# Where the per-token scale of a gated MLP is applied, and one more Strassen product, in a two-layer encoder trunk

## The chip, the core and the metric

The kernel runs on one core of a Trainium2 chip. The metric is the device time of one execution in microseconds (us); lower is better. The engines are called as the profile calls them: PE is TensorE (matrix products), PEld its weight loads, DVE is VectorE, ACT is ScalarE, POOL is GpSimd, and SP issues the DMAs.

## What is computed

The reference is a trunk of two layers over 512 tokens of width 1024. Each layer adds a mixer (differential attention in layer 0, gated linear attention in layer 1, with cross-attention into 256 memory tokens beside it) and then a gated MLP with a causal convolution of width 3. Only the MLP is touched here:

```python
def rms_norm(x, g):
    y = xf * lax.rsqrt(jnp.mean(xf * xf, axis=-1, keepdims=True) + EPS)
    return (y * g)

def conv_ffn(h, w_up, conv_w, conv_b, w_down):
    u = h @ w_up                       # 1024 -> 2 * 2816
    c = depthwise_causal_conv(u, conv_w) + conv_b
    a, g = jnp.split(c, 2, axis=-1)
    return (jax.nn.silu(g) * a) @ w_down
...
        h = rms_norm(x, ffn_norm[i])
        x = x + conv_ffn(h, w_up[i], conv_w[i], conv_b[i], w_down[i])
```

The norm's factor, one number per token, can be applied to the tokens ahead of `w_up` or, since the product is linear, to every result behind it.

## The kernel before

Everything is kept transposed: a tile is 128 features by 512 tokens in float32. The stream `xT[0..7]` is eight such tiles. A factor of a product is split into a high and a low part in the type fp32r (`parts_of`, `split`, `split_weights`: ACT rounds to the high part, DVE subtracts to get the low part), and a product is three matmuls, high by high, high by low, low by high (`product`, lines 407 to 409).

In the MLP (`ffn`) the 2816 hidden features are worked on in eleven groups `q` of 256, the halves `n` of 128 each. For each half there is a linear piece `ua` and a gate piece `ug`; their results stand in one PSUM bank each (`take` deals the eight banks in the order of `TURNS`). `conv` reads a bank: line 1248 multiplies it in place by `rB`, the token factor spread over all partitions, ACT starts the convolution with the middle tap and the bias (1250), and two DVE instructions add the other taps (1251, 1252). Then ACT applies silu to the gate (1455), DVE multiplies (1457), and the hidden tile is split into `mid` parts (1278, 1279). After groups 0 to 3, 4 to 7 and 8 to 10 (`HALVES`) `down` multiplies the hidden tiles into the stream, by Strassen's scheme with seven products of 128 by 256 for what would be eight (line 1358).

Strassen's scheme needs sums of blocks on both sides. Sums of weight blocks are made by POOL (`block_sums`, line 285) and split (308 to 312). Sums of hidden tiles are `mid_sums`, on POOL for most groups and on DVE for the last of a part (line 1286). Sums of tokens are `token_sums`; they need the tokens with the feature gain, made by `scaled` on ACT (line 1321), four POOL subtractions per pair of tiles (1286 with `wsum`), and a split into `vs` parts. `SEVEN` lists the up pieces that use the scheme: groups 5, 6, 8 and 9 of `ua` in each layer and one `ug` piece (`up_by_seven`, line 1233). In such a piece the tiles 6 and 7 go in plainly and the other three pairs of tiles by seven products; four banks hold the partial results, which are combined on ACT and DVE (1238 to 1244). `SUMS_AT` says after which half (2q + n) the sums of which pair of tokens are made.

DVE, ACT and POOL take their instructions from queues in order. The order of PE is the order of the code; the order of the others is set by a planner at build time, which may pull an instruction ahead, except where `keep_in_program_order` fixes it, as on POOL. Weight tiles are made up to six slots ahead (`WB`; a block of a Strassen piece takes two slots, a plain block one), the tag `cvo` has seven buffers, `wsum` two, `vs` twelve, `xs` thirty-six.

Of the kernel before, what the change touches and what calls it, by code (L numbers as in the profile page):

```python
# [14 lines left out]
AF = mybir.ActivationFunctionType  # L15
ALU = mybir.AluOpType
# [69 lines left out]
def _pieces():  # L86
# [3 lines left out]
    def piece(key, name, i, ks, *ranges):  # L90
        plan.append((key, name, i, ks, ranges))

    for l in range(2):
# [24 lines left out]
        for nq in HALVES:  # L118
            for q in range(base, base + nq):
                for key, c in ((("ua", l, q), 256 * q), (("ug", l, q), DFF + 256 * q)):  # L120
                    piece(key, "w_up", l, (6, 7, 4, 5, 0, 1, 2, 3) if key in SEVEN else K8, (c, c + 256))
            for c in range(4):
# [14 lines left out]
    return out  # L137


SEVEN = (('ua', 0, 5), ('ua', 0, 6), ('ua', 0, 8), ('ua', 0, 9), ('ua', 1, 5), ('ua', 1, 6), ('ua', 1, 8), ('ua', 1, 9), ('ug', 0, 9))  # L140
SUMS_AT = {1:(4,5),2:(0,1),3:(2,3)}
TURNS = ('mm', 'mm', 'sm', 'sm', 'lg', 'lg', 'tp', 'tp')


# [40 lines left out]
def trunk(ctx, tc, head_d, x_t, mem_t, wpack, cols_a_d, cols_d, conv_d, gate_d, rel_bias, diff_lambda, consts, onehot, out):  # L185
    nc = tc.nc
    mm = nc.tensor.matmul
    V, A, G = nc.vector, nc.scalar, nc.gpsimd
# [9 lines left out]
    def bank(tag):  # L198
        return ps.tile([128, 512], F32, name=f"ps_{tag}", tag=tag)
# [4 lines left out]
    def split_tiles(pool=None, tag="xs", bufs=XS):  # L204
        pool = pool or xs
        return (pool.tile([128, S], F32R, name=tag + "h", tag=tag, bufs=bufs),
                pool.tile([128, S], F32R, name=tag + "l", tag=tag, bufs=bufs))
# [4 lines left out]
    def blk(b, w=128):  # L212
        return slice(w * b, w * b + w)
# [12 lines left out]
    def tables(name):  # L226
        tc.keep_in_program_order(A.preload_act_table_set(name))
# [94 lines left out]
    def by_seven(i):  # L322
        return plan[i][0][0] == "dn" or plan[i][0] in SEVEN

    def sum_tile():
        return sum_pool[0].tile([128, WTILE], F32, name="wsum", bufs=2)
# [37 lines left out]
    def split(hi, lo, src, gain):  # L364
        A.activation(hi, src, AF.Copy, scale=gain)
        V.scalar_tensor_tensor(lo, src, gain, hi.bitcast(F32), op0=ALU.mult, op1=ALU.subtract)  # L366
# [45 lines left out]
    xT = [None] * KT  # L412
# [12 lines left out]
    def col(i, t=cols):  # L425
        return t[:, i:i + 1]
# [3 lines left out]
    c_ffn = lambda l, k: col(8 * l + k)  # L430
# [70 lines left out]
    with tc.tile_pool(name="ini", bufs=1) as ip, tc.manual_schedule(engines={E.Activation, E.DVE, E.Pool, E.SP}):  # L501
# [8 lines left out]
        p = bank("tp")  # L510
# [48 lines left out]
        for k in range(KT):  # L559
# [17 lines left out]
            hi, lo = parts[k]  # L577
# [590 lines left out]
    def ffn(pool, l, acc):  # L1168
        rB = pool.tile([128, S], F32, name="rB", bufs=1)
        sum_pool[0] = pool  # L1170
        tokens, sums_of, nb = list(zip(xh, xl)), {}, [0]
# [14 lines left out]
        def begin(key):  # L1186
            nonlocal live
            assert plan[used[0]][0] == key, (plan[used[0]][0], key)
            used[0] += 1
            refill()  # L1190
            return used[0] - 1
# [16 lines left out]
        def ctile():  # L1208
            return pool.tile([128, S], F32, name="cvo", bufs=7)

        def up(i, n):
            p, = take(1)
            product(p, whole_piece(i), n, tokens)
            if n == 1:
                release(i, 2, True)
            return p

        def up_by_seven(i):
# [25 lines left out]
            V.tensor_add(b[1], b[1], w)  # L1244
            return b[:2]

        def conv(p, j):
            V.tensor_mul(p, p, rB)
            c = ctile()
            first = A.activation(c, p, AF.Identity, scale=cv[l][:, 2, j:j + 1], bias=cv[l][:, 3, j:j + 1])  # L1250
            V.scalar_tensor_tensor(c[:, 1:], p[:, :S - 1], cv[l][:, 1, j:j + 1], c[:, 1:], op0=ALU.mult, op1=ALU.add)
            final = V.scalar_tensor_tensor(c[:, 2:], p[:, :S - 2], cv[l][:, 0, j:j + 1], c[:, 2:], op0=ALU.mult, op1=ALU.add)
            if later:
                convs[0] += 1
                if convs[0] == (2):
                    convs[0] = 0
                    behind(first, final)
            return c
# [15 lines left out]
        def mid_tile():  # L1274
            return xs.tile([128, S], F32R, name="mid", tag="xs", bufs=XS)

        def parts_of(t, hi, lo):
            A.copy(hi, t)
            V.tensor_sub(lo, t, hi.bitcast(F32))

        def combine(b2, b1, E, t, parts):
            q = [blk(i, 256) for i in range(4)]
            at = lambda i: t[i // 2][:, q[i % 2]] if len(t) > 1 else t[0][:, q[i]]
            for i, x, y in ((0, b1[:, right], b1[:, left]), (1, b2[:, right], at(0)), (2, b2[:, right], b1[:, right]),
                            (3, b2[:, left], at(1))):
                ins = E.tensor_sub(at(i), x, y)  # L1286
                if E is G:
                    tc.keep_in_program_order(ins)
            parts(t)
            return q  # L1290

        def operands(h, lo, bh, bl, fh, fl):
            two = lambda hi, lw, c: (hi[:, c], lw[:, c])
            return [(fh, fl), two(bh, bl, left), two(bh, bl, right), (h[3], lo[3]), (h[0], lo[0]), (h[1], lo[1]),
                    (h[2], lo[2])]
# [16 lines left out]
        def behind(*ins):  # L1312
            with ExitStack() as stack:
                for i in ins:
                    stack.enter_context(tc.issue_after(i.ins))
                while later:
                    parts_of(*later.pop(0))

        def scaled(k):
            t = ctile()  # L1320
            A.activation(t, xT[k], AF.Copy, scale=c_ffn(l, k))
            return t

        def token_sums(ks):
            (bh, bl), (fh, fl) = (tokens[k] for k in ks)
            tiles = [split_tiles(pool, "vs", 12) for _ in range(2)]

            def parts(t):
                for i, (hi, lo) in enumerate(tiles):
                    parts_of(t[0][:, blk(i, S)], hi, lo)  # L1330
            combine(scaled(ks[0]), scaled(ks[1]), G, [sum_tile()], parts)
            h, lo = ([t[i][:, c] for t in tiles for c in (left, right)] for i in range(2))
            sums_of[ks] = operands(h, lo, bh, bl, fh[:, left], fl[:, left])
# [99 lines left out]
        for part, nq in enumerate(HALVES):  # L1433
            mids, pairs = [], []
            last = part == len(HALVES) - 1
            for q in range(base, base + nq):
                c2, ops, at, cs = [], [], {}, {}

                def half(key, n, j):
                    if n == 0:  # L1440
                        at[key] = begin((key, l, q))
                        if (key, l, q) in SEVEN:
                            cs[key] = [conv(p, j + i) for i, p in enumerate(up_by_seven(at[key]))]
                    if key in cs:
                        return lambda: cs[key][n]
                    p = up(at[key], n)
                    return lambda: conv(p, j + n)

                for n in range(2):
                    ua = half("ua", n, 2 * q)  # L1450
                    ug = half("ug", n, 22 + 2 * q)
                    if q == 0 and n == 0:
                        row_scales(acc[0])
                    cn, cg = ua(), ug()
                    A.activation(cg, cg, AF.Silu)
                    end = q == base + nq - 1
                    V.tensor_mul(cn, cn, cg)  # L1457
                    c2.append(cn)
                    if n == 0 or last:
                        ops += [mid_tile(), mid_tile()]  # L1460
                        parts_of(cn, *ops[-2:])
                        pairs.append(ops[-2:])
                    else:
                        m = mid_tile()
                        ops += [m[:, left], m[:, right]]
                        parts_of(cn[:, left], *ops[-2:])
                    if 2 * q + n in SUMS_AT:
                        token_sums(SUMS_AT[2 * q + n])
                if last:
                    ops[2:] = [t[:, left] for t in ops[2:]]  # L1470
                if not last or l == 1:
                    mids.append(mid_sums(c2, ops, V if end else G))
            acc2 = [None]
            if last and l == 0:
                tables("natural_log_exp_and_others")
                gw = gate_raw[0] = ctile()[:96, :384]
                G.memset(gw, 0.0)
                for b in range(3):
                    load(gw[32 * b:32 * b + 17], gate_d)
            down(base, nq, mids, pairs, last, acc2)  # L1480
            base += nq
# [87 lines left out]
```

## Time and profile before

| | |
|---|---|
| median of three runs | 1144.44 us (1144.1 to 1144.5) |
| the profiled execution, its own time | 1144.21 us |
| its span, first to last instruction | 1142.4 us |
| busy: PE, DVE, ACT, POOL | 1137.8, 934.7, 619.8, 279.5 us |
| the MLP of layer 0, of layer 1 (start of first up product to end of last) | 241 to about 559 us, 790 to about 1108 us, then the last `down` |
| granted TensorE clock | 1.0 throughout |

A window of the trace gives for a stretch of time how long each engine was busy in it. Busy time of PE counts a matmul from its start to its modelled end, and matmuls overlap, so the pace of PE is read from the starts in the timeline and not from durations. A group line gives an instruction's line, engine, output and inputs, its shape, its count, its total and mean time, and the idle time ahead of it with what ended that.

### The profile page before, as it was taken

To read this page: it belongs to the slowest core of one execution; us is meant where nothing else is said; L and a number is where in the kernel's file an instruction comes from. 1 tells how busy PE (TensorE), PEld (TensorE's weight loads), DVE (VectorE), ACT (ScalarE), POOL (GpSimd) and SP (SyncE) were. 2 spreads that over 40 slices of the span, in tenths; PEclk is the share of its full clock that TensorE was granted. 3 is DMA by queue.
4 is the path that set the end of the run, shared out by engine and by line. 5 is a ranking of instruction groups with operands and counts; after the bars stand their busy time and mean duration, and the time that the engine had idled before them with its cause. 6 is when DMAs were issued, how large, how long until landed. Compare 5 with 4: busy or idle time off the path is not lost.

```text
span 1142.4 us, 17519 instructions
## 1 busy us (share of the span) xinstructions
PE 1137.8 (100%) x6554; PEld 992.9 (87%) x6554; DVE 934.7 (82%) x1553; ACT 619.8 (54%) x1097; POOL 279.5 (24%) x326
## 2 busy tenths in 40 slices
PE   9999999999999999999999999999999999999998
PEld 7888888888899888999888888988888989899888
DVE  7676778689989899999777636778888988999997
ACT  6676687556554355445557634536664434544552
POOL 0000000004364425760000000000246432575240
PEclk9999999999999999999999999999999999999999
DMA  8522242132313332243252330234222243234312
GB/s 290 175 74 96 79 143 70 59 112 78 125 57 129 100 104 74 89 134 112 88 178 72 94 96 19 82 125 140 74 74 93 93 129 93 92 94 130 105 52 102
DMA packets 39666, 117.87 MB, mean 103 GB/s; under 512 B 4767, under 2 KB 7256, under 8 KB 39582
## 3 DMA queue, kind: packets, MB, share of 16 engines
q1 hardware_dynamic: 39150, 116.37, 32.1%
q8 instruction: 51, 0.84, 0.3%
q10 hardware_dynamic: 432, 0.39, 0.1%
q14 instruction: 33, 0.27, 0.1%
HBM read 112.54 MB, written 4.21 MB: 102 GB/s over the span
## 4 chain that ended last, share of the span: by engine, by line
PE 99%; DMA 0%; DVE 0%; issue 0%; SPq 0%; ACT 0%
PE ps_mm L407 6%; PE ps_mm L408 6%; PE ps_mm L409 6%; PE ps_mm L385 6%; PE ps_mm L387 6%; PE ps_mm L386 6%; PE ps_lg L1358 5%; PE ps_sm L407 4%; PE ps_sm L408 4%; PE ps_sm L409 4%; PE ps_mm L1358 4%; PE ps_tp L1358 4%; PE ps_sm L1358 3%; PE ps_tp L224 3%; PE ps_lg L1233 3%; PE ps_tp L408 3%
## 5 line engine op out<-in xcount | busy, mean ns | idle before, releaser
L260 DVE TENSOR_TENSOR wlo<-raw,whi 128x1024 fp32r<-128x1024 f32 (+5 forms) x165 | 185.9, 1139 | 76.4 <-ACT whi L257 74.2
L257 ACT CAST whi<-raw 128x1024 fp32r<-128x1024 f32 (+5 forms) x165 | 157.2, 967 | 101.2 <-PE ps_mm L408 20.3
L285 POOL TENSOR_TENSOR wsum<-raw 128x256 f32<-128x256 f32 (+1 forms) x112 | 99.6, 910 | 115.2 <-DMA raw<-in_wpack_dram 56.5
L385 PE MATMUL ps_mm<-whi,xsh 128*128 128x512 f32 (+2 forms) x328 | 126.4, 385 | 0.0
L387 PE MATMUL ps_mm<-whi,xsl 128*128 128x512 f32 (+2 forms) x328 | 123.1, 375 | 0.0
L386 PE MATMUL ps_mm<-wlo,xsh 128*128 128x512 f32 (+2 forms) x328 | 122.9, 375 | 0.0
L407 PE MATMUL ps_mm<-xsh,whi 128*128 128x512 f32 x294 | 115.6, 393 | 0.0
L408 PE MATMUL ps_mm<-xsl,whi 128*128 128x512 f32 x294 | 114.7, 390 | 0.0
L409 PE MATMUL ps_mm<-xsh,wlo 128*128 128x512 f32 x294 | 114.6, 390 | 0.0
L311 ACT CAST whi<-wsum 128x1024 fp32r<-128x1024 f32 (+1 forms) x56 | 53.6, 957 | 49.3 <-POOL wsum L285 43.7
L1286 POOL TENSOR_TENSOR cvo<-cvo 128x256 f32<-128x256 f32 x56 | 47.4, 866 | 134.3 <-DVE cvo L1457 133.2
L408 PE MATMUL ps_sm<-xsl,whi 128*128 128x512 f32 x202 | 78.7, 389 | 0.0
L407 PE MATMUL ps_sm<-xsh,whi 128*128 128x512 f32 x202 | 78.7, 389 | 0.0
L409 PE MATMUL ps_sm<-xsh,wlo 128*128 128x512 f32 x202 | 78.6, 389 | 0.0
L312 DVE TENSOR_TENSOR wlo<-wsum,whi 128x1024 fp32r<-128x1024 f32 (+1 forms) x56 | 67.1, 1198 | 7.1 <-ACT whi L311 5.6
L385 PEld LDWEIGHTS ps_mm<-whi,xsh 128*128 128x128 f32 x328 | 61.8, 188 | 11.4 <-issue 1.0
L387 PEld LDWEIGHTS ps_mm<-whi,xsl 128*128 128x128 f32 x328 | 61.7, 188 | 11.3
L386 PEld LDWEIGHTS ps_mm<-wlo,xsh 128*128 128x128 f32 x328 | 61.9, 189 | 10.1
L1263 POOL MEMSET xsh<- 128x128 f32 x2 | 0.4, 210 | 276.4 <-PE ps_sm L408 189.9
L409 PEld LDWEIGHTS ps_mm<-xsh,wlo 128*128 128x128 f32 x294 | 55.2, 188 | 11.6
L407 PEld LDWEIGHTS ps_mm<-xsh,whi 128*128 128x128 f32 x294 | 55.3, 188 | 11.3 <-issue 0.3
L408 PEld LDWEIGHTS ps_mm<-xsl,whi 128*128 128x128 f32 x294 | 55.3, 188 | 11.2 <-DVE xsl L366 0.4
(446 smaller groups left out, 3173.7 us busy)
## 6 DMA issues: line engine op xcount, KB each, us to landing
raw<-in_wpack_dram SPq DMA_DIRECT2D x178, 512.0 KB, 3.6
xt<-in_x_t_dram SPq DMA_DIRECT2D x15, 256.0 KB, 5.1
raw<-in_wpack_dram SPq DMA_DIRECT2D x15, 256.0 KB, 2.9
raw<-in_wpack_dram SPq DMA_DIRECT2D x8, 384.0 KB, 3.3
xres<-xt SPq DMA_DIRECT2D x8, 256.0 KB, 3.4
xt<-xres SPq DMA_DIRECT2D x8, 256.0 KB, 5.5
out_dram<-xt SPq DMA_DIRECT2D x7, 256.0 KB, 2.0
bt<-bias_d SPq DMA_DIRECT2D x6, 256.0 KB, 4.0
```

What stands on the lines that cost most here:

```text
L257: ins = A.copy(hi[:, c], raw[:, c])
L260: V.tensor_sub(lo[:, c], raw[:, c], hi[:, c].bitcast(F32))
L285: tc.keep_in_program_order(getattr(G, "tensor_" + op)(o, x, y))
L311: A.copy(h1[:, m], wsum[:, m])
L312: V.tensor_sub(l1[:, m], wsum[:, m], h1[:, m].bitcast(F32))
L385: mm(p, sh[k][:, blk(b)], hi, start=k == 0, stop=False)
L386: mm(p, sh[k][:, blk(b)], lo, start=False, stop=False)
L387: mm(p, sl[k][:, blk(b)], hi, start=False, stop=k == KT - 1)
L407: mm(p, hi[:, blk(n)], bh, start=i == first, stop=False)
L408: mm(p, hi[:, blk(n)], bl, start=False, stop=False)
L409: mm(p, lo[:, blk(n)], bh, start=False, stop=i == last)
L1358: mm(banks[c][b][:, h], w, v, start=b not in seen[c], stop=m == nq - 1 and t == 2 and i in close)
```

## The change

From the third group on (`q == 2`), the products use the tokens `fresh` in place of `tokens`. `fresh` is made in the first groups: `rescale` multiplies each of the eight stream tiles by `rB` on POOL and splits the result with the feature gain, three tiles after half 0, three after half 1, two after half 2. Their parts lie in the `vs` buffers for tiles 0 to 5. `conv` leaves out the multiplication in the bank when `fresh` is in use. `scaled` makes its tile with gain and `rB` in one DVE instruction in place of ACT's. The token sums are made after halves 4, 5 and 6 in place of 1, 2 and 3, with their parts in `xs` buffers. The linear piece of the fifth group (`q` is 4) in each layer is done by Strassen's scheme, which also changes the order of its weight rows and their sums.

```diff
-SEVEN = (('ua', 0, 5), ('ua', 0, 6), ('ua', 0, 8), ('ua', 0, 9), ('ua', 1, 5), ('ua', 1, 6), ('ua', 1, 8), ('ua', 1, 9), ('ug', 0, 9))
-SUMS_AT = {1:(4,5),2:(0,1),3:(2,3)}
+SEVEN = (('ua', 0, 4), ('ua', 0, 5), ('ua', 0, 6), ('ua', 0, 8), ('ua', 0, 9), ('ua', 1, 4), ('ua', 1, 5), ('ua', 1, 6), ('ua', 1, 8), ('ua', 1, 9), ('ug', 0, 9))
+SUMS_AT = {4: (4, 5), 5: (0, 1), 6: (2, 3)}
+FRESH_AT = {0: (0, 1, 2), 1: (3, 4, 5), 2: (6, 7)}
...
+        fresh = []
+
+        def rescale(ks):
+            for k in ks:
+                t = ctile()
+                tc.keep_in_program_order(G.tensor_mul(t, xT[k], rB))
+                hi, lo = split_tiles(pool, "vs", 12) if k < 6 else split_tiles()
+                split(hi, lo, t, c_ffn(l, k))
+                fresh.append((hi, lo))
+
         def conv(p, j):
-            V.tensor_mul(p, p, rB)
+            if tokens is not fresh:
+                V.tensor_mul(p, p, rB)
...
         def scaled(k):
             t = ctile()
-            A.activation(t, xT[k], AF.Copy, scale=c_ffn(l, k))
+            V.scalar_tensor_tensor(t, xT[k], c_ffn(l, k), rB, op0=ALU.mult, op1=ALU.mult)
             return t
 
         def token_sums(ks):
             (bh, bl), (fh, fl) = (tokens[k] for k in ks)
-            tiles = [split_tiles(pool, "vs", 12) for _ in range(2)]
+            tiles = [split_tiles() for _ in range(2)]
...
             for q in range(base, base + nq):
                 c2, ops, at, cs = [], [], {}, {}
+                if q == 2:
+                    tokens = fresh
...
+                    if 2 * q + n in FRESH_AT:
+                        rescale(FRESH_AT[2 * q + n])
                     if 2 * q + n in SUMS_AT:
                         token_sums(SUMS_AT[2 * q + n])
```

## The prediction

> **What bounds the kernel now.** I read the page's head and its chain first, then the starts of matmuls in the MLP, and only then the load of the other engines.
>
> ```profile
> span 1142.4 us, 17519 instructions
> PE 1137.8 (100%) x6554; PEld 992.9 (87%) x6554; DVE 934.7 (82%) x1553; ACT 619.8 (54%) x1097; POOL 279.5 (24%) x326
> PE 99%; DMA 0%; DVE 0%; issue 0%; SPq 0%; ACT 0%
> ```
>
> The chain that ended last is PE's for 99%: time goes only by making PE's list shorter or by making PE wait. Whether PE keeps its full pace is seen in the timeline of PE (start, duration, instruction), here at the edges of the pieces of group 5:
>
> ```profile
> 390.62 0.39 PE L407 MATMUL ps_lg<-xsh,whi 128*128 128x512 f32 x1
> 400.54 0.28 PE L1233 MATMUL ps_lg<-vsh,whi 128*128 128x256 f32 x1
> 400.66 0.28 PE L1233 MATMUL ps_lg<-vsl,whi 128*128 128x256 f32 x1
> 400.90 0.40 PE L407 MATMUL ps_mm<-xsh,whi 128*128 128x512 f32 x1
> 401.13 0.40 PE L408 MATMUL ps_mm<-xsl,whi 128*128 128x512 f32 x1
> 411.80 0.39 PE L407 MATMUL ps_sm<-xsh,whi 128*128 128x512 f32 x1
> ```
>
> From start to start a matmul of 512 columns takes 0.23 us and one of 256 columns 0.12. The plain `ug` piece, 48 matmuls, goes from 400.90 to 411.80: 10.90, which is 48 times 0.227. The Strassen piece before it, 12 matmuls of 512 and 63 of 256, goes from 390.62 to 400.90: 10.28. Both are the bare sum of their matmuls, so there is no wait to be taken away here. DVE is the engine next to its limit: in the stretch from the first token factors to the use of the last hidden tiles of the first part, in layer 0 and in layer 1 (windows; the engines in the order PE, PEld, DVE, ACT, POOL):
>
> ```profile
> 252.60:341.10 88.50, 88.50 (x441) 75.49 (x440) 80.57 (x104) 51.59 (x74) 40.00 (x44) 1.00 0.25 79
> 801.60:890.00 88.40, 88.40 (x442) 75.39 (x441) 79.05 (x104) 52.71 (x75) 37.33 (x44) 1.00 0.25 78
> ```
>
> DVE is idle for 7.9 us of 88.5, and 9.4 of 88.4.
>
> **PE's list.** A plain `ua` piece is 48 matmuls of 512. By seven, three of its four pairs of tiles go from 12 matmuls of 512 (12 x 0.227 = 2.72) to 21 of 256 (21 x 0.120 = 2.52). From the rows above the piece shortens by 10.90 - 10.28 = 0.6 us, and the change has two such pieces, one in each layer: 1.2 us off the path, since PE is the path. Counted by columns alone it would be more: a pair would save 3 of 24 units of 0.1135, for six pairs 2.0 us; the rows take 0.120 for 256 columns where half of 0.227 is 0.1135, and that eats the rest. The Trainium skill, page "TensorE: Matmul & The Clock Gate", section "Back-to-back issue gap", gives 518 and 262 cycles for 512 and 256 columns; by these the saving would be an estimated 1.8 us. The trace is slower at both widths, and I take the rows.
>
> **DVE from the third group on.** The multiplication in the bank, all four banks' worth in each layer:
>
> ```profile
> L1248 DVE TENSOR_TENSOR ps_sm<-ps_sm,rB x28: 680/691/700, 262.4 to 1108.7; 128x512 f32<-128x512 f32 x28
> L1248 DVE TENSOR_TENSOR ps_mm<-ps_mm,rB x26: 682/690/702, 256.3 to 1097.4; 128x512 f32<-128x512 f32 x26
> L1248 DVE TENSOR_TENSOR ps_lg<-ps_lg,rB x18: 682/689/693, 272.4 to 1060.0; 128x512 f32<-128x512 f32 x18
> L1248 DVE TENSOR_TENSOR ps_tp<-ps_tp,rB x16: 682/684/694, 282.0 to 1087.3; 128x512 f32<-128x512 f32 x16
> ```
>
> They are 88, four in each of 22 groups. Nine groups of eleven lose theirs: 36 in a layer, 36 x 0.69 = 24.8 us of DVE. Off the path, because PE waits for none of it.
>
> The new work, by the nearest rows: the low part of a fresh tile is the same instruction as `split` makes for the old ones, and `scaled` on DVE has that form too (two tiles and a column).
>
> ```profile
> L366 DVE SCALAR_TENSOR_TENSOR xsl<-xt,cols,xsh 128x512 fp32r<-128x512 f32 x16 | 12.0, 747 | 0.8 <-ACT xsh L365 0.8
> L1321 ACT ACTIVATE cvo<-xt,cols 128x512 f32<-128x512 f32 x12 | 8.0, 713 | 0.0
> ```
>
> A layer gets 8 + 6 of them, 14 x 0.747 = 10.5 us, and ACT gives 6 x 0.713 back and takes 8 splits, which at half load it can. All 14 fall into the stretch of the two windows, but only groups 2 and 3 lose their multiplication there: 8 x 0.69 = 5.5. The splits of token sums move from groups 0 and 1 to 2 and 3 inside the stretch, at no change in it. So DVE gets 5.0 us more: 85.5 of 88.5, and 84.0 of 88.4. The relief comes only behind it.
>
> Behind it the fifth group costs DVE the combination of the banks (four of the first row here, two of the second, 3.0 us) and larger splits of weights (two plain blocks against one of 896 with 512 and one of 768 with 1024 columns):
>
> ```profile
> L1242 DVE TENSOR_TENSOR cvo<-cvo,ps_tp x4: 405/413/416, 406.0 to 1057.9; 128x256 f32<-128x256 f32 x4
> L1243 DVE TENSOR_TENSOR ps_sm<-ps_sm,cvo 128x512 f32<-128x512 f32 x2 | 1.4, 692 | 0.0
> L260 DVE TENSOR_TENSOR wlo<-raw,whi 128x1024 fp32r<-128x1024 f32 x125 | 153.0, 1237 | 67.3 <-ACT whi L257 65.4 <-PE ps_lg L790 1.3
> L260 DVE TENSOR_TENSOR wlo<-raw,whi 128x896 fp32r<-128x896 f32 x9 | 11.4, 1265 | 1.7 <-ACT whi L257 1.5
> L309 DVE TENSOR_TENSOR wlo<-raw,whi 128x768 fp32r<-128x768 f32 x44 | 49.7, 1130 | 0.6 <-ACT whi L308 0.6
> L312 DVE TENSOR_TENSOR wlo<-wsum,whi 128x512 fp32r<-128x512 f32 x12 | 10.7, 890 | 3.1 <-PE ps_lg L1233 1.6 <-ACT whi L311 1.5
> L312 DVE TENSOR_TENSOR wlo<-wsum,whi 128x1024 fp32r<-128x1024 f32 x44 | 56.4, 1282 | 4.0 <-ACT whi L311 4.0
> ```
>
> That is 1.265 + 0.890 + 1.130 + 1.282 - 2 x 1.237 = 2.1, with the banks 5.1 us, against 28 x 0.69 = 19.3 us that groups 4 to 10 lose. I cost it at nothing; its cover is those 19.3 us.
>
> **POOL's eight multiplications.** No row shows one of 512 columns. The cost on POOL is bounded by two of 256, alone and crowded; DVE's side is in the rows below them (timeline, then groups of the first window):
>
> ```profile
> 317.30 1.43 POOL L1286 TENSOR_TENSOR cvo<-cvo 128x256 f32<-128x256 f32 x2
> 321.60 2.36 POOL L285 TENSOR_TENSOR wsum<-raw 128x256 f32<-128x256 f32 x2
> 323.28 1.22 DVE L1457 TENSOR_TENSOR cvo<-cvo 128x512 f32<-128x512 f32 x1
> 339.08 1.28 DVE L1279 TENSOR_TENSOR mid<-cvo,mid 128x512 fp32r<-128x512 f32 x2
> L1279 DVE TENSOR_TENSOR mid<-cvo,mid 128x512 fp32r<-128x512 f32 x12 | 9.9, 852 | 0.0
> L1457 DVE TENSOR_TENSOR cvo<-cvo 128x512 f32<-128x512 f32 x8 | 6.8, 852 | 1.7 <-ACT cvo L1455 1.5
> L1279 DVE TENSOR_TENSOR vsl<-wsum,vsh 128x512 fp32r<-128x512 f32 x6 | 5.8, 963 | 2.1 <-ACT vsh L1278 2.1
> ```
>
> On POOL 1.4 to 2.4 us each, 11 to 19 us a layer, on an engine that is idle for 48 of 88. They wait for `rB` and a `cvo` buffer; behind them queue the hidden sums of groups 0 and 1, whose use is tens of us away. The last pair of fresh tiles has from group 1's first half to PE's start of group 2, 10 us, so I put that at nothing.
>
> But DVE pays: its 512-column instruction takes about 0.68 (two in 1.28) while POOL is idle and 1.22 beside POOL. Over the window the three groups lie above 0.68 by 12 x 0.17 + 8 x 0.17 + 6 x 0.28 = 5.1 us, for 44 POOL instructions: 0.12 each. Eight of double width: 1.9 us. That is the low end (none at all would need POOL and DVE never to meet); the high end is that each holds DVE for all of 1.43, 11.4 us. I take 1.9, as the one row that counts met and unmet ones together: DVE then has 87.4 of 88.5, and 85.9 of 88.4. It fits, with nothing to spare.
>
> **What is late next if it does not fit.** DVE's last duty of the stretch is the parts of group 3's hidden tiles, 339.08 + 1.28 = 340.36; PE takes them here:
>
> ```profile
> 342.20 0.40 PE L1358 MATMUL ps_sm<-mid,whi 128*128 128x256 f32 x2
> 342.92 0.40 PE L1358 MATMUL ps_sm<-mid,whi 128*128 128x256 f32 x2
> ```
>
> The first tile stands at 339.76 for 342.20, the second at 340.36 for 342.92: 2.4 us to spare. The chain to them also loses the last bank's multiplication, 0.7. So DVE may come 3.1 us late before PE waits.
>
> **The sum.** Profiled execution: 1142.4 - 1.2 = 1141.2 of span, plus the 1.8 around it, 1143.0. The median shown lies 0.2 above the profiled time: **1143.2 us**. A measurement here tells about 0.2%, 2.3 us, from no change; the forecast lies inside it.
>
> **Rivals.**
> (A) Slower: POOL's multiplications hold DVE. From 85.5 us, DVE meets the limit at 88.5 + 3.1, so this decides from 6.1 us in eight, 0.76 us each; in layer 1 from 7.5. With 2 x (1.22 - 0.68) = 1.08 each, 8.6 in all, PE waits 2.5 and 1.1: 1146.8. With the full 1.43, 11.4, it waits 5.3 and 3.9: 1152.4. Against it is the mean of 0.12; for it, that a wide multiplication meets DVE more surely when DVE has no idle time left. The middle is 1149.6. The Trainium skill, page "SBUF — State Buffer", section "SBUF: two separate sides", says that the port pair of the two engines is an exclusive lock held for the whole instruction. By that rule the full hold is the price; the 1.22 agrees with it, and no row here shows the width in question.
> (B) Slower: the two `wsum` buffers, seen in these rows:
>
> ```profile
> 325.18 1.33 POOL L285 TENSOR_TENSOR wsum<-raw,wsum 128x256 f32<-128x256 f32 x1
> 327.58 1.21 DVE L312 TENSOR_TENSOR wlo<-wsum,whi 128x1024 fp32r<-128x1024 f32 x1
> 329.10 1.05 ACT L311 CAST whi<-wsum 128x1024 fp32r<-128x1024 f32 x1
> 331.61 1.21 DVE L312 TENSOR_TENSOR wlo<-wsum,whi 128x1024 fp32r<-128x1024 f32 x1
> 336.08 0.40 PE L1358 MATMUL ps_lg<-mid,whi 128*128 128x256 f32 x2
> ```
>
> The token sums now want one while the sums for `down` want both. The second block of those starts at 321.60 and would have to wait for the first one's split, the L312 that frees it at 328.8; its own four sums take 4.9, its splits 2.3, so 336.0 before queueing, against PE's use at 336.08 (the first of `ps_lg`). With a couple of us of queueing, 2.5 a layer: 1148.2. Against it: that split ends at 332.82 now, 3.3 us early.
> (C) Faster than forecast: by columns 2.0 saved, 1142.4, and a little elsewhere. Against it is that PE waits nowhere in these stages.
>
> **How the numbers follow.** Forecast 0.58; A 0.27; B 0.11; C 0.04, of which 0.03 beyond 0.2%. Hence faster 0.03, same 0.59, slower 0.38. The range goes from C's 1142.4 to 1151.5, which leaves out A's top and less than 0.2 in all; the forecast's own range is 1142.4 to 1146.7.
>
> **What would show it.** The piece of group 4 should last 10.28 in place of 10.90 in both layers; edges of plain pieces should stay 10.88 to 10.90 apart; line 1248 should appear 16 times. DVE's busy time in the first window near 87. A gap of PE at the first part's `down`, with DVE's last split past 342, is A; one with its weights' split late is B. A wait of PE at the start of group 2, for a fresh tile, would prove my zero there wrong.

## The result and the profile after

The median went from 1144.43 to 1155.28 us (1155.14 to 1155.52): ratio 1.0096, interval 1.0078 to 1.0113, so 10.85 us slower. The forecast was 1143.2 with a range up to 1151.5; the time lies above the range. The profiled execution took 1155.14 us, with a span of 1153.2. One execution of a later run, with only the token sums moved, had a granted clock of 0.19 throughout and is left out of its median.

The page's head and its chain of the changed kernel; lines of the code have moved by 12 or so (1248 is now 1260, 1279 is 1291, 1286 is 1298, 1358 is 1370, 285 is 286, 311 and 312 are 312 and 313, 407 to 409 are 408 to 410):

```profile
span 1153.2 us, 17680 instructions
PE 1141.5 (99%) x6608; PEld 996.4 (86%) x6608; DVE 936.2 (81%) x1525; ACT 621.5 (54%) x1107; POOL 340.3 (30%) x358
PE 83%; DVE 13%; issue 1%; POOL 1%; ACT 1%; DMA 0%; SPq 0%; DVEq 0%; ACTq 0%; POOLq 0%
```

DVE's share of the chain rose from 0% to 13%, though its busy time rose by only 1.5 us and its load went from 82 to 81%. PE now waits. Where, the distances between the starts of matmuls tell, beyond 0.227 us for 512 columns and 0.120 for 256: 6.5 us in layer 0 and 5.5 in layer 1, together 12.0; less the forecast's 1.2 this is 10.8, the whole of the difference between the two spans. In layer 0 they are 0.6 at the start of group 2 (290), 4.5 in the first `down` (337 to 343) and 1.3 behind it; in layer 1, 3.2 and 1.6 at the first `down`, 0.6 behind it. Timeline of PE at the start of group 2 and in the first `down`, after:

```profile
290.62 0.50 PE L409 MATMUL ps_mm<-xsl,whi 128*128 128x512 f32 x1 [0.35 <-DVE xsl L367]
...
337.12 0.28 PE L1370 MATMUL ps_lg<-mid,wlo 128*128 128x256 f32 x1
339.12 0.50 PE L1370 MATMUL ps_lg<-mid,whi 128*128 128x256 f32 x2 [1.73 <-ACT whi L312]
340.50 0.58 PE L1370 MATMUL ps_lg<-mid,wlo 128*128 128x256 f32 x1 [0.87 <-DVE wlo L313]
```

It isn't the hidden tiles that come late first, as the forecast's budget had it, but the weight sums of `down`. Back along their chain (POOL, then ACT, then DVE, three answers of the timeline):

```profile
329.57 1.19 POOL L1298 TENSOR_TENSOR wsum<-cvo,wsum 128x256 f32<-128x256 f32 x1
333.39 2.38 POOL L286 TENSOR_TENSOR wsum<-raw 128x256 f32<-128x256 f32 x2 [2.63 <-DVE wlo L313]
```
```profile
338.02 1.04 ACT L312 CAST whi<-wsum 128x1024 fp32r<-128x1024 f32 x1 [3.82 <-POOL wsum L286]
```
```profile
332.10 1.21 DVE L313 TENSOR_TENSOR wlo<-wsum,whi 128x1024 fp32r<-128x1024 f32 x1
333.24 0.68 DVE L1291 TENSOR_TENSOR xsl<-wsum,xsh 128x512 fp32r<-128x512 f32 x1
334.50 0.68 DVE L1291 TENSOR_TENSOR xsl<-wsum,xsh 128x512 fp32r<-128x512 f32 x1
339.10 1.34 DVE L313 TENSOR_TENSOR wlo<-wsum,whi 128x1024 fp32r<-128x1024 f32 x1 [1.85 <-ACT whi L312]
```

POOL cannot begin the next weight sum until DVE's split at 332.10 gives a `wsum` buffer back; it begins at 333.39, ACT rounds at 338.02, DVE splits at 339.10, and PE, which wanted the tile from 337.24, gets its low part at 340.50. The other buffer holds a token sum meanwhile (329.57). Before, the two splits of weight sums stood at 327.58 and 331.61 (in the rows shown for B), 4.5 and 7.5 us earlier. In the last microseconds ahead of the deadline DVE makes the token splits (`xsl<-wsum`) of group 4's Strassen piece, which PE uses only from 375.

The first window in six parts shows the shift. The two rows that matter, before (us, busy PE, PEld, DVE, ACT, POOL; clock; DMA):

```profile
274.10:295.90 21.80, 21.80 (x98) 18.04 (x97) 20.20 (x25) 14.21 (x22) 11.83 (x12) 1.00 0.28 87
328.50:341.10 12.60, 12.60 (x106) 12.57 (x105) 11.77 (x18) 6.66 (x10) 7.64 (x8) 1.00 0.24 68
```

And after:

```profile
274.10:295.90 21.80, 21.45 (x94) 17.23 (x94) 20.65 (x28) 11.62 (x18) 6.17 (x6) 1.00 0.42 128
328.50:341.10 12.60, 10.00 (x76) 9.44 (x75) 10.75 (x12) 5.73 (x8) 9.82 (x9) 0.96 0.27 83
```

POOL's work moved from groups 0 and 1 to the end of the part, and PE made 76 matmuls in the last window where it had made 106.

### The profile page after: what moved, and what is told of

Read it like the earlier page. It is cut to its first block, busy times and chain, and to the rows that moved or that the text cites. A ratio compares the mean times of both kernels' runs of the same rounds, so it can differ in the third digit from the quotient of the medians.

```text
span 1153.2 us, 17680 instructions
## 1 busy us (share of the span) xinstructions
PE 1141.5 (99%) x6608; PEld 996.4 (86%) x6608; DVE 936.2 (81%) x1525; ACT 621.5 (54%) x1107; POOL 340.3 (30%) x358
## 4 chain that ended last, share of the span: by engine, by line
PE 83%; DVE 13%; issue 1%; POOL 1%; ACT 1%; DMA 0%; SPq 0%; DVEq 0%; ACTq 0%; POOLq 0%
PE ps_mm L386 6%; PE ps_mm L388 6%; PE ps_mm L387 6%; PE ps_mm L409 4%; PE ps_mm L408 4%; PE ps_mm L410 4%; PE ps_sm L408 4%; PE ps_sm L409 4%; PE ps_sm L410 4%; PE ps_tp L1370 3%; PE ps_lg L408 3%; PE ps_lg L410 3%; PE ps_lg L409 3%; PE ps_lg L1370 3%; PE ps_tp L225 3%; PE ps_tp L1234 3%
## 5 line engine op out<-in xcount | busy, mean ns | idle before, releaser
L286 POOL TENSOR_TENSOR wsum<-raw 128x256 f32<-128x256 f32 (+1 forms) x120 | 115.7, 985 | 93.4 <-DMA raw<-in_wpack_dram 32.0
L1469 ACT ACTIVATE cvo<-cvo 128x512 f32<-128x512 f32 x44 | 27.8, 632 | 81.8 <-DVE cvo L1264 81.8
L386 PEld LDWEIGHTS ps_mm<-whi,xsh 128*128 128x128 f32 x328 | 61.7, 188 | 11.4 <-issue 1.0
L388 PEld LDWEIGHTS ps_mm<-whi,xsl 128*128 128x128 f32 x328 | 61.7, 188 | 11.3
L1290 ACT CAST mid<-cvo 128x512 fp32r<-128x512 f32 x82 | 46.8, 578 | 41.8 <-DVE cvo L1471 33.2
L1291 DVE TENSOR_TENSOR mid<-cvo,mid 128x512 fp32r<-128x512 f32 x82 | 63.7, 794 | 5.6 <-ACT mid L1290 5.3
L286 POOL TENSOR_TENSOR wsum<-wsum,raw 128x256 f32<-128x256 f32 (+1 forms) x60 | 62.6, 1044 | 0.0
L408 PE MATMUL ps_mm<-xsh,whi 128*128 128x512 f32 x150 | 59.5, 397 | 0.0
L409 PE MATMUL ps_mm<-xsl,whi 128*128 128x512 f32 x150 | 58.7, 392 | 0.4 <-DVE xsl L367 0.4
L410 PE MATMUL ps_mm<-xsh,wlo 128*128 128x512 f32 x150 | 58.5, 390 | 0.0
L286 POOL TENSOR_TENSOR wsum<-raw,wsum 128x256 f32<-128x256 f32 (+1 forms) x60 | 56.0, 934 | 4.7
L1370 PE MATMUL ps_tp<-mid,whi 128*128 128x256 f32 x272 | 53.4, 286 | 0.1
```

The source lines that it names most:

```text
L286: tc.keep_in_program_order(getattr(G, "tensor_" + op)(o, x, y))
L386: mm(p, sh[k][:, blk(b)], hi, start=k == 0, stop=False)
L388: mm(p, sl[k][:, blk(b)], hi, start=False, stop=k == KT - 1)
L408: mm(p, hi[:, blk(n)], bh, start=i == first, stop=False)
L409: mm(p, hi[:, blk(n)], bl, start=False, stop=False)
L410: mm(p, lo[:, blk(n)], bh, start=False, stop=i == last)
```

## The experiments

Times are medians against the kernel before on the same chip (1144.1 to 1144.3 there); "waits" are PE's, layer 0 / layer 1, counted by starts as above, lowered clock included. The theories at the outset: (1) the two `wsum` buffers, my rival B; (2) POOL's eight multiplications, my rival A; (3) the second half of the change, the fifth group.

### Taking one suspect away from the changed kernel

**Own buffers for the token sums.**
```diff
-                    parts_of(t[0][:, blk(i, S)], hi, lo)
-            combine(scaled(ks[0]), scaled(ks[1]), G, [sum_tile()], parts)
+                    parts_of(t[i], hi, lo)
+            combine(scaled(ks[0]), scaled(ks[1]), G, [xtile(), xtile()], parts)
```


> The changed kernel with one edit: the sums of tokens are made in two tiles of the tag xs instead of in a wsum tile, so that only weight sums use the two wsum buffers; the order on POOL is the same, and DVE and POOL have the same work. Theory 1 (buffers, rival B): the waits of PE at the first down of each layer go, about 4.4 to 5.7 us in layer 0 and 5.6 in layer 1; 1144 to 1147 us, and PE's wait of 0.7 us at the start of group 2 stays. Theory 2 (DVE overfull by POOL's multiplications, rival A): nothing that loads DVE has changed, so 1153 us or more and the same gaps.

Measured 1154.0, 1.0086 [1.0072, 1.0100]: 1.3 us better. Waits 5.5 / 5.9. The chain of buffers that the timeline shows is there, but with it cut DVE is late for the same tiles all the same. Timeline of ACT, then of DVE, in this run, and a row of its windows:

```profile
335.47 1.05 ACT L312 CAST whi<-wsum 128x1024 fp32r<-128x1024 f32 x1 [1.98 <-POOL wsum L286]
```
```profile
338.69 1.21 DVE L313 TENSOR_TENSOR wlo<-wsum,whi 128x1024 fp32r<-128x1024 f32 x1
```
```profile
322.00:341.00 19.00, 16.67 (x105) 15.03 (x104) 18.89 (x20) 7.72 (x11) 18.69 (x18) 0.96 0.17 55
```

ACT has rounded the sum at 336.52, 2.5 us earlier than in the changed kernel, but DVE, busy for 18.89 of 19.00 us there, gets to the split only 0.4 us earlier. POOL is as full, with 18.69. B as the main cause falls.

**No multiplication on POOL.** The token factor is then missing from groups 2 to 10.
```diff
-                t = ctile()
-                tc.keep_in_program_order(G.tensor_mul(t, xT[k], rB))
+                t = xT[k]
```


> The changed kernel without POOL's eight multiplications by rB in each layer; the fresh tokens are split from the unscaled stream, so the scale is left out of groups 2 to 10. Theory 1 (buffers): only the wait at the start of group 2 may go, 1154 to 1155 us. Theory 2 (POOL's multiplications hold DVE): DVE gets 2 to 9 us back in each layer ahead of down, and most of the waits go, 1144 to 1149 us.

Measured 1147.96, 1.0035 [1.0021, 1.0048]: 7.3 better, waits 2.4 / 2.9. Windows, with the fresh tiles cheap:

```profile
252.60:274.10 21.50, 21.50 (x97) 17.80 (x96) 19.70 (x27) 12.36 (x16) 2.62 (x4) 1.00 0.32 98
274.10:295.90 21.80, 21.80 (x98) 18.06 (x97) 18.94 (x25) 11.54 (x16) 3.52 (x6) 1.00 0.33 97
```

DVE has 38.6 us of work in groups 0 and 1 here against 20.57 + 20.65 = 41.2 in the changed kernel. A is real, but 2.4 to 2.9 us a layer stay without it. The edit also takes away the wait for POOL's result and eight uses of a `cvo` buffer in a layer, so the 7.3 us are the price of the whole step and not of POOL and DVE meeting alone.

**The fifth group as before** (`SEVEN` of the kernel before).

> The changed kernel with the linear piece of the fifth group done plainly, as before the change. Both theories: the waits stand ahead of the fifth group and stay, PE has 1.2 us more to do, 1156 to 1157 us. If the larger weight splits of the fifth group's Strassen piece are what is late at down, the time falls below 1155 instead.

Measured 1156.17, 1.0106 [1.0092, 1.0120]: 0.9 worse, with the same waits (6.55 / 5.5). The two pieces pay what they should; theory 3 falls.

**The gain of the sums on ACT again**, without the token factor there.
```diff
-            V.scalar_tensor_tensor(t, xT[k], c_ffn(l, k), rB, op0=ALU.mult, op1=ALU.mult)
+            A.activation(t, xT[k], AF.Copy, scale=c_ffn(l, k))
```


> The changed kernel with the token tiles of the sums made on ACT as before the change, without rB (the scale is left out of the token sums): six DVE instructions of about 0.75 to 1.2 us less in each layer, in groups 2 and 3; POOL's multiplications stay. If the cause is that DVE is overfull whatever the source, 4.5 us less a layer takes most of the wait away: 1146 to 1150 us. If only POOL's hold in groups 0 and 1 counts, 1153 us or more.

Measured 1149.49, 1.0043 [1.0028, 1.0059]: 5.8 better for 6 instructions of 0.95 us in a layer, 11.4 in all. Waits 3.7 / 2.8.

**Two together, then three.** POOL's multiplications and the shared buffers away; then the sums' gain on ACT as well.

> Both edits together: POOL's multiplications left out (the scale is missing from groups 2 to 10) and the sums of tokens in two xs tiles. If the wsum buffers are a second cause that was hidden behind DVE's load, 1143.5 to 1145.5 us. If they do not matter, 1148 us as without the multiplications alone.

> The changed kernel without POOL's multiplications, with the token tiles of the sums made on ACT without rB, and with the sums in xs tiles; the scale is missing from groups 2 to 10. DVE has about what it had before ahead of the first down (eight splits more, eight multiplications less). If DVE's load there is the whole cause: no wait of PE, and the 1.2 us of the fifth group's pieces are seen, 1143 us. If moving the token sums into groups 2 and 3 costs by itself: 1145 us or more.

Measured 1147.12 (1.0024 [1.0015, 1.0034]) and 1146.76 (1.0022 [1.0013, 1.0032]); waits in the last 1.7 / 2.3. The single gains, 7.3 + 5.8 + 1.3, would be 14.4, more than there was to lose; together they make 8.5. What stays in the last one seems to have another cause. Timeline of POOL, then of ACT, there:

```profile
326.65 1.71 POOL L1297 TENSOR_TENSOR xt<-cvo,xt 128x256 f32<-128x256 f32 x1
328.33 2.44 POOL L286 TENSOR_TENSOR wsum<-raw 128x256 f32<-128x256 f32 x2
```
```profile
333.03 1.05 ACT L312 CAST whi<-wsum 128x1024 fp32r<-128x1024 f32 x1 [3.28 <-POOL wsum L286]
333.98 0.77 ACT L1261 ACTIVATE cvo<-ps_tp,cv 128x512 f32<-128x512 f32 x1
```

POOL makes the token sums ahead of the weight sums for `down`; ACT waits 3.28 us for these, and the reading of the last bank stands behind that in ACT's queue. Even with all three suspects gone the sums are in the way, so their place in time became the suspect.

**The multiplication on DVE.**
```diff
-                tc.keep_in_program_order(G.tensor_mul(t, xT[k], rB))
+                V.tensor_mul(t, xT[k], rB)
```


> The changed kernel with the eight multiplications on DVE instead of POOL: DVE gets 8 x 0.69 = 5.5 us of work in each layer in place of what POOL takes from it. If POOL's multiplications cost by holding DVE about as long as they last (1.3 us or more each), the time falls by several us, to 1146 to 1151 us. If they cost DVE less than its own 0.69 us each, the time stays or rises: 1155 to 1160 us.

Measured 1169.1, 1.0217 [1.0203, 1.0230]: 13.8 worse than the changed kernel, waits 12.6 / 14.0. Sixteen instructions cost 0.86 us each more on DVE than on POOL, the lower clock included: PE ran at half clock for 20.5 us (13.7 and 6.8), which by the distances of its starts lost about 7 us, against 1.3 in the changed kernel.

### Adding one part to the kernel before

**The fifth group alone.**
```diff
-SEVEN = (('ua', 0, 5), ('ua', 0, 6), ...
+SEVEN = (('ua', 0, 4), ('ua', 0, 5), ('ua', 0, 6), ...
```


> The kernel before with only the fifth group's linear piece done by Strassen's scheme, the scale still multiplied in the banks. If the saving of 0.6 us a piece is right and DVE's 5.1 us more find room without the relief: 1143.2 us. If the relief of DVE was needed for it, PE waits in groups 4 to 6: 1145 us or more.

Measured 1146.89, 1.0024 [1.0013, 1.0034]: 2.7 slower instead of 1.2 faster. PE's waits there:

```profile
PE ps_mm L1358 <- DVE mid L1279: 1.4, 3, 0.7
...
PE ps_sm L1358 <- DVE wlo L312: 0.7, 2, 0.4
```

**Eight multiplications on POOL whose results nobody uses**, in the places of `rescale`.
```diff
+        def idle_mul(ks):
+            for k in ks:
+                tc.keep_in_program_order(G.tensor_mul(ctile(), xT[k], rB))
...
+                    if 2 * q + n in FRESH_AT:
+                        idle_mul(FRESH_AT[2 * q + n])
```


> The kernel before, with POOL's eight multiplications by rB added after the same halves in each layer into cvo tiles that nobody reads. Theory A (POOL holds DVE): DVE has 7.9 us idle and 2.4 us of slack in the first part of layer 0, 9.4 and 2.4 in layer 1; eight full holds of 1.4 us, 11.4 us, would give PE a wait of about 1 us in layer 0: 1144.5 to 1146 us, with DVE's busy time in the first window near 88 of 88.5. At 0.24 us a multiplication: 1144.2 us and about 82.5 busy.

Measured 1146.76, 1.0021 [1.0012, 1.0030]: 2.6 us for 16, 0.16 each. DVE's time above the shortest instruction of each line and form in the stretch rose from 8.2 to 10.9 us in layer 0 and from 7.6 to 11.1 in layer 1.

**Idle multiplications on DVE in groups 2 and 3, then in group 2 alone.**
```diff
+            if j % 22 // 2 in (2, 3):      # then: in (2,)
+                V.tensor_scalar(p, p, 1.0, None, op0=ALU.mult)
```


> The kernel before, with each bank of groups 2 and 3 multiplied by 1.0 on DVE once more: eight instructions of 0.6 to 0.69 us a layer, in PSUM, beside the same POOL work; 5 to 5.5 us of DVE a layer ahead of the first down. If DVE's idle time is room (my budget: 80.6 + 5.5 of 88.5), nothing waits: 1144.2 us. If the idle time is round trips to ACT that no work can fill, only the 2.4 us by which the last splits are early is room: PE waits about 3 us a layer, 1149 to 1151 us.

> The same in group 2 alone: four instructions, 2.4 to 2.8 us a layer. If idle time is room: 1144.2 us. If the room is 2.4 us: 1144.2 to 1145.5 us. If there is no room at all: 1149 us.

Measured 1156.28, 1.0106 [1.0091, 1.0121], for 2 x 5.5 us more on DVE: 12.2 slower. And 1147.86, 1.0036 [1.0024, 1.0048], for 2.4 to 2.8 in a layer: 3.8 slower, waits 1.45 / 2.15. So DVE, idle for 7.9 and 9.4 us of the stretch, had room for some 0.7 us a layer at this place. These instructions stand between a bank and ACT's reading of it, so they also lengthen that chain; what room there is for work beside the chain no run tells.

**Only the token sums moved.**
```diff
-SUMS_AT = {1:(4,5),2:(0,1),3:(2,3)}
+SUMS_AT = {4: (4, 5), 5: (0, 1), 6: (2, 3)}
```


> The kernel before with one edit: the token sums after halves 4, 5 and 6 instead of 1, 2 and 3, still made on ACT and still without the scale, which stays in the banks. DVE, ACT and POOL have the same work, only later. If the place of the sums costs by itself (POOL makes them ahead of the weight sums for down, and ACT's queue stands behind those): PE waits 1 to 3 us a layer at the first down, 1146 to 1150 us. If only more work on DVE costs: 1144.2 us.

Measured 1161.94, 1.0150 [1.0134, 1.0167]: 17.7 us slower, more than the whole change. The kernel was run again for a profile.

> The kernel of e13 once more for a trace that can be read. If POOL's order is what holds up the first down: the sums of weights for down start late, behind the last token sums and the wsum buffers, ACT's rounding of them and the reading of group 3's last bank stand behind that, and PE's waits lie at the first down of both layers, about 8 us each.

1161.93 there, waits 8.5 / 9.5. No token factor on POOL, no `scaled` on DVE, no fresh tile, the same amount of work as before. The line of the splits (`vsl`), before:

```profile
L1279 DVE TENSOR_TENSOR vsl<-wsum,vsh x6: 678/952/1255, 271.2 to 296.9; 128x512 fp32r<-128x512 f32 x6
```

and with the sums moved (its windows, and PE in the first `down`, follow):

```profile
L1279 DVE TENSOR_TENSOR vsl<-wsum,vsh x6: 692/1222/1254, 304.0 to 330.3; 128x512 fp32r<-128x512 f32 x6
```
```profile
274.10:295.90 21.80, 21.80 (x98) 18.06 (x97) 16.57 (x23) 10.22 (x14) 2.94 (x4) 1.00 0.34 97
328.50:341.10 12.60, 10.87 (x79) 10.27 (x78) 11.60 (x14) 6.23 (x9) 10.98 (x11) 0.90 0.27 83
```
```profile
348.18 0.38 PE L1358 MATMUL ps_sm<-mid,whi 128*128 128x256 f32 x1 [2.27 <-ACT mid L1278]
349.01 0.58 PE L1358 MATMUL ps_sm<-mid,whi 128*128 128x256 f32 x1 [0.44 <-DVE mid L1279]
```

The six splits moved from 271-297 to 304-330. In 274.1 to 295.9 DVE lost 3.6 us of work and simply stood idle: no work of groups 2 and 3 exists yet to fill that. In the last window POOL rose from 7.64 to 10.98 of 12.6.

What had been expected of this run, weight sums of `down` that start late behind the last token sums, is in its timeline of POOL too. The same sums began at 321.60 before (in the rows shown for POOL's eight multiplications):

```profile
328.45 1.18 POOL L1286 TENSOR_TENSOR wsum<-cvo,wsum 128x256 f32<-128x256 f32 x1
331.08 2.42 POOL L285 TENSOR_TENSOR wsum<-raw 128x256 f32<-128x256 f32 x2 [1.46 <-DVE vsl L1279]
```

So two things came with the moved sums: the splits on DVE, six in a layer, and twelve subtractions on POOL, of which the last four stand ahead of these weight sums in its queue. No run moves the one without the other.

**The same with the sums in buffers of their own** (the first edit above, with two `ctile()`).

> The kernel of e13 with the sums of tokens in two cvo tiles in place of a wsum tile. If the two wsum buffers are what makes the moved sums costly: most of the 17.8 us goes, 1146 to 1151 us. If it is the work itself in those groups, on POOL and DVE: 1158 us or more.

Measured 1159.49, 1.0132 [1.0115, 1.0149]: 2.4 better, 15.3 above before. B is a small part here too.

### The sums at other times, and none at all

**The last sums one half later** (`6: (2, 3)` becomes `7: (2, 3)`), **then all behind group 4** (after halves 8, 9 and 10, with `ua` of groups 6 to 10 by seven in place of 4, 5, 6, 8, 9).

> The changed kernel with the token sums of tiles 2 and 3 made after half 7 instead of 6: two DVE tiles, four POOL subtractions and two splits less stand ahead of group 3's hidden tiles. If DVE's load ahead of the first down decides: 3 to 4 us a layer less of it, 1148 to 1151 us. If those sums are then late for the fifth group or hold up down's own sums, 1154 us or more.

> The changed kernel with its sums after halves 8, 9 and 10, where DVE no longer multiplies in the banks, and Strassen's scheme for the linear pieces of groups 6 to 10 instead of 4, 5, 6, 8 and 9 (the same number). If the waits come from putting sums and their splits into the two groups ahead of the first down: no wait there, and the two additional pieces are seen, 1143 us. If the fresh tokens alone already make the first down wait: 1146 us or more.

Measured 1163.28 (1.0168 [1.0151, 1.0185]), waits 11.4 / 9.4; and 1163.23 (1.0162 [1.0147, 1.0177]). In the second the first part waits 0.9 / 0.0 us, which supports the cause; but the later parts wait instead: about 7 us in the second `down` of layer 0, 6 in that of layer 1, and 6 more in layer 1's third. The collision follows the sums. This second version doesn't compute what the reference does, for a reason that I don't know, so its times are weaker evidence than the others.

**No Strassen pieces and no sums**, in the changed kernel and in the kernel before (`SEVEN = ()`, `SUMS_AT = {}`).

> The changed kernel with every up piece done plainly, hence without any token sums: what is left of the change is the fresh tokens, POOL's multiplications among them, and the banks that are no longer multiplied. Beside the run of the kernel before with the same cut: equal if the fresh tokens alone fit where the token sums were, 2 us or more slower if they do not.

> The kernel before with every up piece done plainly and without token sums: PE has nine pieces of 0.6 us more, 1149.5 us, and no wait.

Measured 1150.40 (1.0050 [1.0034, 1.0067]) and 1149.21 (1.0042 [1.0027, 1.0057]). Without sums the fresh tokens cost 1.2 us, of which 0.7 is one wait of PE at the start of group 2 in layer 0; the other half microsecond I can't place. So nearly all of the loss needs the sums. And the kernel before loses 4.9 us without its nine pieces, where nine times 0.6 would be 5.4.

No version here beats the kernel before.

## Why the prediction was wrong

**The step that failed** is in the part on DVE: "The splits of token sums move from groups 0 and 1 to 2 and 3 inside the stretch, at no change in it." Moved alone, the token sums with these splits cost 17.7 us. Two errors stand behind it. I added up DVE's work over all 88.5 us and compared it with 88.5; and I took its idle time as room. But work of group 2 can't begin before its banks are full, so what is freed in groups 0 and 1 is lost, and the idle time of groups 2 and 3 is made of short waits in a chain of ACT and DVE, which extra work lengthens instead of filling. That is how I read the rows and the runs with idle instructions; no run shows the chain by itself. In 295.9 to 341.1 of the kernel before, groups 2 and 3 of layer 0, DVE was idle for 3.9 of 45.2 us: 2.0 of it waiting for ACT's middle tap and 1.5 for the silu.

```profile
L1251 DVE SCALAR_TENSOR_TENSOR cvo<-ps_lg,cv,cvo 128x511 f32<-128x511 f32 x2 | 1.5, 750 | 1.2 <-ACT cvo L1250 1.2
L1251 DVE SCALAR_TENSOR_TENSOR cvo<-ps_mm,cv,cvo 128x511 f32<-128x511 f32 x2 | 1.5, 742 | 0.8 <-ACT cvo L1250 0.8
L1457 DVE TENSOR_TENSOR cvo<-cvo 128x512 f32<-128x512 f32 x5 | 4.3, 867 | 1.6 <-ACT cvo L1455 1.5
```

**The sum as it should have been made**, from 295.9 to 341.1, where it is decided, with a room that only the run with four idle instructions told. DVE by groups in that window, after (the first two kinds are new there but for one split):

```profile
L1291 DVE TENSOR_TENSOR xsl<-wsum,xsh 128x512 fp32r<-128x512 f32 x6 | 5.7, 955 | 0.0
...
L1333 DVE SCALAR_TENSOR_TENSOR cvo<-xt,cols,rB 128x512 f32<-128x512 f32 x6 | 5.6, 953 | 0.0
...
L1471 DVE TENSOR_TENSOR cvo<-cvo 128x512 f32<-128x512 f32 x3 | 3.6, 1193 | 0.8 <-ACT cvo L1469 0.8
```

The kernel before has there eight multiplications in banks (5.5 us) and one split (0.7). So DVE goes from 6.2 to 11.3 us in these kinds: 5.1 more, less the room of 0.7, 4.4 a layer. The measured waits are 6.5 and 5.5, and 1.3 of the first is PE at half clock (below): 5.2 and 5.5. By this sum the profiled time would have been 1144.2 - 1.2 + 8.8 = 1151.8; of the 3.3 us up to 1155.1 the clock is 1.3. For the other 2.0 the trace has a candidate: the instructions that both kernels have in this window take 3.4 us longer after than by their means before, the silu product (L1471) 1.19 us against 0.87, while POOL is busy for 35.6 us in place of 24.4. That these meet POOL more often is an argument; no run shows it apart.

POOL's queue is the rival that this account leaves. With the buffers parted DVE was still the late one, and a lighter DVE alone won back 5.8 us with POOL's order as it was; with all three suspects gone waits of 1.7 and 2.3 stayed, while the token sums stood ahead of `down`'s weight sums on POOL. In the kernel with only the sums moved the two shares aren't known.

**The other steps.** The PE term was right: the piece of group 4 goes from 375.30 to 385.60, 10.30 against my 10.28 (timeline of PE, after), and the kernel with both pieces done plainly again was 0.9 us slower.

```profile
375.30 0.40 PE L408 MATMUL ps_mm<-xsh,whi 128*128 128x512 f32 x1
```
```profile
385.60 0.40 PE L408 MATMUL ps_lg<-vsh,whi 128*128 128x512 f32 x1
```

The multiplication in the bank appears 16 times, as said. The zero for the fifth group's work on DVE was right as far as its cover goes, and the cover is needed: without the relief the same pieces cost 2.7 us in place of a gain of 1.2. The zero at the start of group 2 was wrong, by 0.6 us in layer 0. The row that I named as a sign, DVE near 87 us in the first window, came out at 31.16 + 51.62 = 82.8 (two rows of windows, after): an engine that comes late has done less by a fixed time, so it was the wrong sign to ask for.

```profile
252.60:285.00 32.40, 32.40 (x144) 26.85 (x143) 31.16 (x40) 21.55 (x29) 16.20 (x12) 1.00 0.21 65
285.00:341.10 56.10, 53.15 (x264) 44.65 (x263) 51.62 (x60) 27.04 (x40) 35.61 (x35) 0.99 0.27 85
```

**The rivals.** A had the right sign and half the story. My price for it, 0.12 us each, was near what the kernel before pays (0.16); in the changed kernel the same step is worth 7.3 / 16 = 0.46 for each. It leaves DVE 2.6 us more to do in groups 0 and 1 of layer 0, and DVE no longer has time to lose. It does not decide only from 0.76 each, as I had put it: the runs with idle instructions found, in groups 2 and 3, a room not of 6.1 us but of less than one. The rule of the Trainium skill in "SBUF — State Buffer", section "SBUF: two separate sides" (an exclusive lock between the two engines), I had turned into a full hold of 1.43 each. A single meeting comes near it, in the timeline of DVE in the changed kernel:

```profile
263.06 1.78 DVE L367 SCALAR_TENSOR_TENSOR vsl<-cvo,cols,vsh 128x512 fp32r<-128x512 f32 x1
289.83 0.73 DVE L367 SCALAR_TENSOR_TENSOR xsl<-cvo,cols,xsh 128x512 fp32r<-128x512 f32 x1
```

An instruction of the same form takes 0.73 us alone and 1.78 there, beside a multiplication on POOL, so the trace agrees with the rule for an instruction that meets; as a mean over all eight no run shows that much. B is seen in the timeline and worth 1.3 to 2.4 us, my figure of 2.5 a layer being twice to four times too high. The sign that I had named for it, a late split of weights at `down`, was there and stayed with the buffers parted, so it could not tell B from a late DVE. C played no part.

## What to carry to other kernels

Cost a moved piece of work where it lands, stretch by stretch up to the next deadline, and not over a window that contains both its old and its new place. Idle time of an engine that works in a chain with another need not be room: try it with a few idle instructions of known length (here 2.6 us a layer cost 1.9, and 5.5 cost 6.1, both inside the chain). Single removals don't add where several things are late for the same tile, so the test that decides is the one that puts one part into the kernel before.

## What the runs showed of the hardware

A few waits of PE lowered its clock. After, windows around the first `down`:

```profile
336.00:340.00 4.00, 1.90 (x14) 1.49 (x12) 2.15 (x3) 1.73 (x2) 3.92 (x5) 1.00 0.20 46
340.00:343.40 3.40, 2.90 (x13) 2.90 (x14) 2.61 (x4) 1.35 (x2) 3.32 (x5) 0.51 0.25 100
```

PE was busy for 1.90 of 4.00 us, and then the granted clock was 0.51 for 3.4 us. From 340.5 to 343.4 the starts of matmuls of 256 columns lie 0.21 us apart in place of 0.12, about 1.3 us lost on top of the waits. With only the sums moved the clock was low for 3.4 + 3.4 + 6.8 us, by the starts about 5 us of that kernel's 17.7. The rest, 12.6, is what its twelve moved splits take at their new place (12 x 1.05 us), but POOL's share is in it too, so that they come out equal shows nothing by itself. The Trainium skill, "TensorE: Matmul & The Clock Gate", section "What's actually happening", has half clock after an idle window of about 3.4 us. The duration of the lowered clock agrees, 3.4 us or twice that in these two kernels; but here no pause was that long, and PE's pauses of 1.73 and 0.87 us with matmuls in between were enough.
